# Two transformer blocks in float32: background work timed by a model of the engines, lower parts of weights on VectorE alone

## The chip, the cores and the metric

The kernel runs on one core of one Trainium2 chip. The metric is the device time of one execution in microseconds (us); the median of several runs is compared. The engines of the core each work through a queue of their own, in order: TensorE (PE in the profile; its weight loads are PEld), VectorE (DVE), ScalarE (ACT), GpSimd (POOL) and SyncE (SP), which issues most DMAs.

## The reference

512 tokens of 1024 features pass through two blocks, all in float32:

```python
h = rmsnorm(x, g_pre[l, 0]) * (1 + sc1) + sh1
x = x + 0.5 * gt1 * rmsnorm(swiglu(h, w_gu1[l], w_dn1[l]), g_post[l, 0])
h = rmsnorm(x, g_pre[l, 1]) * (1 + sc2) + sh2
y = token_mixer(h, w_in[l], w_a2[l], b_a[l], b_f[l], g_gla[l], w_pa[l], w_pb[l], w_out[l])
x = x + gt2 * rmsnorm(y, g_post[l, 1])
h = rmsnorm(x, g_pre[l, 2]) * (1 + sc3) + sh3
x = x + 0.5 * gt3 * rmsnorm(swiglu(h, w_gu2[l], w_dn2[l]), g_post[l, 2])
```

The mixer of block 1 is gated linear attention (4 heads) beside a softmax attention with forget gates (16 heads). Block 2 has the same three sub-layers, without the norm on a sub-layer's output; its mixer is a sparse attention of 8 heads (compressed keys, selected and window branch) beside retention of 8 heads. `swiglu` has 2816 hidden features. A last norm gives the result.

## The kernel before

**Products in parts.** Every float32 operand of a weight product is split in two: `hi`, rounded to the format of TensorE's fast pass, and `lo`, the rest. A product is three: hi hi, hi lo, lo hi. Weights come as slabs of 4 x 128 rows by 256 columns (512 KB). For a slab `dma` (L232) loads it to one of 4 buffers `raw`, and `split` (L245) makes its parts: ScalarE casts `hi` (L252), then the *lower part* `lo = raw - hi` (L254) is made by VectorE, or by GpSimd if the job works on half of the tokens (`j_half`). There are 5 pairs of `hi` and `lo`. While a norm has its `hold`, GpSimd's lower parts are kept in `later`, until `catch_up` (L262).

**One order, made in Python.** Instructions are issued engine by engine in the order of the program text, with no reordering. `run` (L298) goes through the list of jobs (a slab and its products); `feed` (L268) loads and splits the slabs ahead. After each three products it calls `background` (L219), which advances Python generators (norms, attention, modulation) whose time has come. Time is `vt`, the sum of what TensorE's products cost; a generator that yields 2.0 goes on when TensorE has been given 2 us more of products. `vt` knows no waits. The numbers are the constants at the top (L24 to L34). `wait_flag` (L226) advances a generator at once where a job needs its result.

**Changes of sub-layer.** The last products of a sub-layer (`tail`) run on tokens 0 to 255 and then on 256 to 511, and so do the first of the next (`head`). So the norm of the first half stands beside the products of the second, and the norm of the second beside the next sub-layer's first half. In block 1 the norm is `residual1` (L525: `rstd`, then for eight chunks of features the scaling L532, the addition to x L538, the square L482 or L485 on ScalarE and its sum L491 in `flush`), then `prenorm` (L494: `rstd` again, then L511, ScalarE's L512 and the lower part L502 for each chunk). In block 2 it is `prenorm` alone. `rstd` (L441) yields Y1, multiplies the sums by ones (TensorE, through `mm`, L184), scales (VectorE, L454), takes the power -1/2 (GpSimd, L456), yields Y2 and spreads the factor over the partitions (TensorE again). The first products of a head go chunk by chunk, each as its chunk of `h` is there.

**Attention.** `softmax_seq` (L1490) serves both softmax attentions: per call the scores of four token tiles (L184), their bias and row minimum on VectorE (L1521), the exponentials on ScalarE (L1524), the scaling by the row sums (L1533), transposes (L189) with copies out on ScalarE and VectorE (L1564, L1562), and the products with the values (`weighted`, L1572). `ret_pair` makes retention for two heads: DMAs that turn rows, rotations (L1858 to L1860), scores, their decay (L1875), values, norm. `gla` (L1266) makes linear attention. All yield fixed numbers between these steps. All products that are not a job's go through `mm` (L183) or `transpose` (L187) to the four banks `bp`; those of jobs through `mmr` (L179) to the banks `mp`. Results of a SwiGLU product are taken out at L566 and L574.

Of the kernel before, what the change touches and what calls it, by code (L numbers as in the profile page):

```python
# [14 lines left out]
ALU = mybir.AluOpType  # L15
# [3 lines left out]
T = 512  # L19
# [4 lines left out]
YR, YP = 1.0, 0.8  # L24
Y1, Y2 = 2.0, 2.0
# [3 lines left out]
S1, SN, S2, S3 = 1, 3, 0.6, 0.4  # L29
KS, NS = 2, 8  # L30
R1, R2, R3 = 4, 1, 0.6
LS, GH = 2, 4
# [57 lines left out]
def packed(name, a, slabs):  # L90
    """The weight a, slab after slab, each with its rows of a chunk on the partitions."""
# [26 lines left out]

class Core:
    def __init__(self, ctx, tc, inp, out):  # L120
        self.tc, self.nc, self.inp, self.out = tc, tc.nc, inp, out
# [11 lines left out]
        self.nraw = self.hold = 0  # L133
# [13 lines left out]
    def alloc(self, rounded=False):  # L147
        """A [128, 512] tile. rounded: for a part of a product's operand (never for other values)."""
# [30 lines left out]
    def mmr(self, out, lhsT, rhs, start, stop):  # L179
        self.nc.tensor.matmul(out, r_(lhsT), r_(rhs), start=start, stop=stop)  # L180
        self.vt += max(0.108, 0.000422 * self.cols(rhs))

    def mm(self, out, lhsT, rhs, start=True, stop=True):  # L183
        self.nc.tensor.matmul(out, lhsT, rhs, start=start, stop=stop)  # L184
# [34 lines left out]
    def background(self):  # L219
        n = 0  # L220
        while self.step(self.vt):
# [19 lines left out]
    def slot(self, old):  # L241
        """A pair of tiles for the parts of a slab that no job from number old on uses."""
        return next((i for i in sorted(range(len(self.his)), key=lambda q: self.until[q]) if self.until[i] < old), None)

    def split(self, j, i):  # L245
# [7 lines left out]
        j_half = j.t1 - j.t0 < T  # L253
        low = lambda e: e.tensor_tensor(r_(l), r, h, op=ALU.subtract)  # L254
# [12 lines left out]

    def feed(self, i):  # L268
        """Loads and splits of the slabs that job i and the next ones use, as far as there is memory."""
# [4 lines left out]
        while moved:  # L274
            moved = False
            if (self.nd < len(L) and self.nd < self.ns + len(self.raws) and L[self.nd] < i + DMA_AHEAD
                    and not any(q.raw is self.raws[self.nraw % len(self.raws)] for q, _ in self.later)):
# [10 lines left out]
    def plan(self):  # L288
        """Which jobs load their slab, and until which job its parts are in use."""
# [8 lines left out]
    def run(self):  # L298
        J = self.jobs
        prev = None  # L300
        for i, j in enumerate(J):
# [11 lines left out]
            if any(q in (j, j.like, prev) for q, _ in self.later):  # L313
                self.catch_up()
# [61 lines left out]
    def turn(g, back=True):  # L376
        """The jobs of a pair by their chunks, from the last to the first or from the first to the last."""
# [6 lines left out]
    def emit_units(self, units, head=0, tail=0, need=None, after=None):  # L384
        """units: lists of pairs. The first `head` and the last `tail` units run on the two halves of the
        tokens one after the other. need: flags (half A, half B); after(t0, t1): called when a half is through."""
# [5 lines left out]
        def both(us):  # L392
            """The jobs of the two halves, the second in the opposite order, so that it finds parts of slabs."""
# [21 lines left out]
                # the first two pairs slab by slab, so that they use the first chunks as soon as they are there  # L415
# [25 lines left out]
    def rstd(self, acc, t0, t1, n=D, eps=EPS):  # L441
        """Generator: sums acc over the partitions, returns 1/sqrt(mean + eps) of each token on all partitions
        (a PSUM bank)."""
        nc = self.nc
        self.flush(acc)
        self.hold += 1
        yield Y1
# [9 lines left out]
        self.hold -= 1  # L457
        if not self.hold:
            self.catch_up()
        yield Y2  # L460
# [16 lines left out]
    def sumsq(self, acc, src, t0, t1, first):  # L477
        """acc += src * src on tokens t0..t1 (square on ScalarE, sum on VectorE, one call later)."""
# [15 lines left out]
    def prenorm(self, acc, h, a, b, t0, t1, flag, spill=False):  # L494
        """Generator: h = (x * a) * rstd + b, split into the parts of h."""
# [13 lines left out]
        for c in range(KC):  # L509
# [6 lines left out]
            yield YP  # L516
# [8 lines left out]
    def residual1(self, y, accy, accx, coef, h, a, b, t0, t1, flag, spill=False):  # L525
        """Generator: x += coef * rmsnorm(y); then the next h from x."""
# [1476 lines left out]
```

## Time and profile before

| | us |
|---|---|
| median of 3 runs (2731.23 to 2737.29) | 2735.96 |
| span of the profiled execution | 2734.5 |
| TensorE busy | 2627.8 |
| VectorE busy | 1403.1 |
| ScalarE busy | 993.9 |
| GpSimd busy | 620.6 |

The profile has no time of its own for that execution beside its span. A line of a group gives the source line, engine, operation, the tile written and those read, shapes, the count, the busy time in us, the mean in ns of one, and then the time for which the engine stood idle just before it, with what released it. A line of waits gives the waiting engine and line, the releaser, the total in us, how often, and the longest. The granted clock (PEclk) is a share of TensorE's full clock.

### The profile page before, as it was taken

How to read it: one execution, taken by the hardware profiler on the slowest of the kernel's cores; microseconds unless marked ns; L12 is line 12 of the kernel's file. 1: busy time of each engine (PE TensorE's matmuls, PEld its weight loads, DVE VectorE, ACT ScalarE, POOL GpSimd, SP SyncE). 2: the span in 40 equal slices, each digit the busy share in tenths (PEclk: the TensorE clock that was granted, in tenths of full speed). 3: DMA queues.
4: the chain of work that ended last, by engine and by line, in shares of the span. 5: the costliest groups of instructions: out<-in, count | busy, mean ns of one | idle time of the engine just before them, and what ended most of it. 6: DMA issues, size and time to landing. Idle time of an engine off the chain costs nothing. (4 is left out here: it accounts for less than half of the span.)

```text
span 2734.5 us, 37488 instructions
## 1 busy us (share of the span) xinstructions
PE 2627.8 (96%) x14965; PEld 2236.6 (82%) x14965; DVE 1403.1 (51%) x2176; ACT 993.9 (36%) x1688; POOL 620.6 (23%) x472
## 2 busy tenths in 40 slices
PE   6999999999999998899998999999999999999998
PEld 4888898888877788888888988899857669998888
DVE  6678446684335535468857333333455454633322
ACT  3332234444344434432234322234345224432223
POOL 4111054430111114411145300044000103520014
PEclk8999999999999999999999999999999999999999
DMA  6677334212333323377843323235310323342323
GB/s 225 220 249 269 101 112 134 79 40 83 126 108 112 97 89 128 115 256 266 277 161 117 111 100 108 94 99 188 101 39 32 123 78 123 116 139 85 108 86 100
DMA packets 128915, 355.12 MB, mean 130 GB/s; under 512 B 16365, under 2 KB 38838, under 8 KB 128740
## 3 DMA queue, kind: packets, MB, share of 16 engines
q1 hardware_dynamic: 110180, 285.54, 31.5%
q0 software_dynamic: 18560, 67.18, 7.2%
q8 instruction: 117, 1.92, 0.3%
q14 instruction: 58, 0.48, 0.1%
HBM read 343.20 MB, written 6.32 MB: 128 GB/s over the span
## 5 line engine op out<-in xcount | busy, mean ns | idle before, releaser
L180 PE MATMUL mp<-t,hi 128*128 128x512 f32 (+1 forms) x7936 | 2047.7, 348 | 11.8 <-DVE t L801 3.6
L180 PEld LDWEIGHTS mp<-t,hi 128*128 128x128 f32 x7936 | 1383.6, 192 | 201.2 <-issue 17.2
L180 PE MATMUL mp<-t,lo 128*128 128x512 f32 (+1 forms) x3968 | 1371.4, 346 | 0.1
L180 PEld LDWEIGHTS mp<-t,lo 128*128 128x128 f32 x3968 | 759.8, 191 | 90.9 <-POOL lo L254 0.3
L252 ACT CAST hi<-raw 128x1024 fp32r<-128x1024 f32 (+2 forms) x493 | 486.1, 991 | 595.8 <-PE mp L180 362.3
L254 DVE TENSOR_TENSOR lo<-raw,hi 128x1024 fp32r<-128x1024 f32 (+3 forms) x316 | 369.4, 1175 | 560.2 <-ACT hi L252 557.7
L254 POOL TENSOR_TENSOR lo<-raw,hi 128x1024 fp32r<-128x1024 f32 (+1 forms) x177 | 401.9, 2285 | 938.5 <-ACT hi L252 919.2
L881 DVE SCALAR_TENSOR_TENSOR big<-big,sc,big 128x1024 f32<-128x1024 f32 x112 | 145.6, 1300 | 22.9 <-DMA big<-in_w_ada 12.5
L180 PE MATMUL mp<-hi,t 128*128 128x256 f32 x704 | 137.5, 291 | 0.0
L574 DVE TENSOR_TENSOR t<-mp,t 128x512 f32<-128x512 f32 (+1 forms) x77 | 44.8, 595 | 152.4 <-PE mp L180 152.4
L180 PEld LDWEIGHTS mp<-hi,t 128*128 128x128 f32 x704 | 114.3, 195 | 6.6 <-issue 5.8
L184 PE MATMUL bp<-t,t 128*128 128x128 f32 (+11 forms) x618 | 111.7, 411 | 6.8 <-DVE t L1875 3.3
L1113 ACT CAST t<-t 128x512 fp32r<-128x512 f32 (+1 forms) x89 | 49.0, 556 | 176.3 <-DVE t L574 160.8
L491 DVE TENSOR_TENSOR t<-t,t 128x256 f32<-128x256 f32 (+1 forms) x109 | 89.9, 827 | 27.2 <-ACT t L485 26.5
L180 PE MATMUL mp<-lo,t 128*128 128x256 f32 x352 | 100.9, 287 | 0.0
L1122 ACT ACTIVATE t<-mp 128x512 f32<-128x512 f32 (+1 forms) x103 | 54.1, 543 | 126.0 <-PE mp L180 123.4
L184 PEld LDWEIGHTS bp<-t,t 128*64 128x64 f32 (+3 forms) x618 | 59.0, 166 | 46.3 <-issue 30.5
L1486 POOL TENSOR_TENSOR big<-big,cmask 128x128 f32<-128x128 f32 x64 | 33.9, 531 | 233.4 <-DMA big<-fdram 233.3
L566 ACT ACTIVATE t<-mp 128x512 f32<-128x512 f32 (+1 forms) x79 | 40.7, 523 | 119.9 <-PE mp L180 119.9
L1524 ACT ACTIVATE t<-t,smx 128x512 f32<-128x512 f32 (+3 forms) x117 | 65.1, 558 | 51.4 <-DVE smx L1521 51.0
L875 POOL DMA_DIRECT2D big<-in_ada_w x72 | 38.8, 539 | 189.0 <-DVE big L881 103.8
L485 ACT ACTIVATE t<-t 128x256 f32<-128x256 f32 (+1 forms) x108 | 44.9, 423 | 97.6 <-DVE t L961 40.4
(269 smaller groups left out, 1774.1 us busy)
## 6 DMA issues: line engine op xcount, KB each, us to landing
raw<-in_w_in SPq DMA_DIRECT2D x112, 512.0 KB
raw<-in_ffn_w_in SPq DMA_DIRECT2D x102, 512.0 KB
raw<-in_w_gu SPq DMA_DIRECT2D x89, 512.0 KB
big<-in_ada_w POOLq DMA_DIRECT2D x72, 512.0 KB, 5.1
big<-in_w_ada POOLq DMA_DIRECT2D x56, 512.0 KB, 4.9
raw<-in_w_dn SPq DMA_DIRECT2D x42, 512.0 KB
raw<-in_ffn_w_out SPq DMA_DIRECT2D x42, 512.0 KB
raw<-in_w_out SPq DMA_DIRECT2D x22, 512.0 KB
```

Source lines behind the costliest of these rows:

```text
L180: self.nc.tensor.matmul(out, r_(lhsT), r_(rhs), start=start, stop=stop)
L184: self.nc.tensor.matmul(out, lhsT, rhs, start=start, stop=stop)
L252: self.nc.scalar.copy(r_(h), r)
L254: low = lambda e: e.tensor_tensor(r_(l), r, h, op=ALU.subtract)
L485: nc.scalar.activation(s[:, t0:t1], src[:, t0:t1], AF.Square)
L491: self.nc.vector.tensor_tensor(acc[:, t0:t1], acc[:, t0:t1], s[:, t0:t1], op=ALU.add)
L566: nc.scalar.activation(s[c, t0][:, t0:t1], banks[n][:, t0:t1], AF.Silu)
L574: nc.vector.tensor_tensor(t[:, tk], banks[n][:, tk], t[:, tk], op=ALU.mult)
L881: nc.vector.scalar_tensor_tensor(acc, raw, self.sc[blk][:, k:k + 1], acc, op0=ALU.mult, op1=ALU.add)
L1113: self.nc.scalar.copy(r_(hi[:, tk]), t[:, tk])
L1122: self.nc.scalar.activation(d[2 * i + n][:, t0:t1], banks[n][:, t0:t1], AF.Copy, scale=scale or 1.0)
L1524: nc.scalar.activation(r, r, AF.Exp, bias=mn[:, c:c + 1], scale=-1.0, accum_out=sm[:, c:c + 1])
```

## The change

Three things change together.

1. Yields. The fixed numbers of norms, softmax, linear attention (in part) and retention go. A class `Times` keeps, for every 128 columns of every tile, when they are expected to be made and last used, and when each engine is free, from a cost for each instruction; `Timed` and `Engine` (not shown in full) pass each instruction on and enter it there. A generator yields until its operands are expected (`when`), a bank `bp` is expected to be free (`bank`), or VectorE is at most 0.7 us ahead of TensorE (`room`).
2. `vt` is TensorE's time by the same model, with its waits; a product of 256 columns counts 0.120 us and not 0.108, and two that use different parts of the array run beside each other.
3. Lower parts. All go to VectorE, in order through `later`: each is issued as soon as its `hi` is expected, or when a job needs it. `hold` is gone. The parts in `startup` (L719) stay on GpSimd.

The other yields (GS, CS, KS, LS, RET_STEP, AD, AP and plain numbers) stay. The rest of the diff takes out comments.

```diff
-YR, YP = 1.0, 0.8
-Y1, Y2 = 2.0, 2.0
...
-S1, SN, S2, S3 = 1, 3, 0.6, 0.4
...
-R1, R2, R3 = 4, 1, 0.6
-LS, GH = 2, 4
+LS = 2
...
+class Times:
+    LAG = {"PE": 0.2, "DVE": 0.15, "ACT": 0.16, "POOL": 0.15}
+    COST = {"DVE": (0.07, 1 / 960), "ACT": (0.09, 1 / 1200), "POOL": (0.12, 2.2e-3)}
+    def __init__(self):
+        self.free = {"PE": 0.0, "DVE": 0.0, "ACT": 0.0, "POOL": 0.0, "SP": 0.0}
+        self.made, self.used = {}, {}
+        self.lock = {"DVE": 0.0, "POOL": 0.0}
+        self.dma = 0.0
+        self.log = None
+    @staticmethod
+    def keys(ap):
+        row = ap.ap[0][0] or 1
+        at = ap.offset % row
+        n = at + sum(abs(s) * (c - 1) for s, c in list(ap.ap)[1:])
+        return [(ap.tensor.tag, q) for q in range(at // 128, n // 128 + 1)]
+    @staticmethod
+    def on_chip(ap):
+        return hasattr(ap, "tensor") and hasattr(ap.tensor, "tag") and ap.space != bass.MemoryType.DRAM
+    def ready(self, *aps):
+        return max((self.made.get(k, 0.0) for a in aps for k in self.keys(a)), default=0.0)
+    def start(self, engine, outs, ins):
+        t = self.free.get(engine, 0.0)
+        for a in ins:
+            for k in self.keys(a):
+                t = max(t, self.made.get(k, 0.0))
+        for a in outs:
+            for k in self.keys(a):
+                t = max(t, self.used.get(k, 0.0))
+        return t
+    def finish(self, outs, ins, end, lag):
+        for a in ins:
+            for k in self.keys(a):
+                self.used[k] = max(self.used.get(k, 0.0), end)
+        for a in outs:
+            for k in self.keys(a):
+                self.made[k] = end + lag
+                self.used[k] = max(self.used.get(k, 0.0), end)
+    def run(self, engine, op, outs, ins, n, two):
+        base, per = self.COST[engine]
+        cost = base + per * n
+        if engine == "POOL" and "memset" in op:
+            cost = 0.1 + n / 1200
+        if engine == "POOL" and n <= 8:
+            cost = 0.7
+        if op in ("scalar_tensor_tensor", "tensor_tensor_reduce", "tensor_tensor_scan"):
+            cost += 0.06
+        if engine == "ACT" and two:
+            cost += 0.09
+        psum = any(a.space == bass.MemoryType.PSUM for a in ins + outs)
+        t = self.start(engine, outs, ins)
+        both = len(ins) > 1 and not psum and not (engine == "ACT")
+        if engine == "DVE" and len(ins) > 1 and sum(a.free_size() > 1 for a in ins) > 1 and not psum:
+            t = max(t, self.lock["POOL"])
+            self.lock["DVE"] = max(self.lock["DVE"], t + cost)
+        elif engine == "POOL" and ins:
+            t = max(t, self.lock["DVE"])
+            self.lock["POOL"] = t + cost
+        self.free[engine] = t + cost
+        self.finish(outs, ins, t + cost, self.LAG[engine])
+        if self.log is not None:
+            self.log.append((engine, op, t, cost))
+    def load(self, engine, out, in_):
+        t = self.free[engine]
+        outs, ins = [a for a in (out,) if self.on_chip(a)], [a for a in (in_,) if self.on_chip(a)]
+        t = self.start(engine, outs, ins)
+        self.free[engine] = t + (0.37 if engine == "SP" else 0.54)
+        n = 1
+        for q in out.shape:
+            n *= q
+        self.dma = max(self.dma, t + 1.6) + 4e-6 * n / 0.33
+        self.finish(outs, ins, self.dma, 0.3)
+        if self.log is not None:
+            self.log.append((engine, "dma", t, 0.4))
...
+    def pe(self, out, lhsT, rhs, cost, part=None):
+        t = self.times.start("PE", [out], [lhsT, rhs])
+        before, at = self.beside
+        if part and before and not part & before:
+            t = max(self.times.start(None, [out], [lhsT, rhs]), at)
+            part = None
+        self.beside = part, t
+        self.vt = self.times.free["PE"] = max(self.vt, t + cost)
+        self.times.finish([out], [lhsT, rhs], t + cost, self.times.LAG["PE"])
+        if self.times.log is not None:
+            self.times.log.append(("PE", "mm", t, cost))
     def mmr(self, out, lhsT, rhs, start, stop):
         self.nc.tensor.matmul(out, r_(lhsT), r_(rhs), start=start, stop=stop)
-        self.vt += max(0.108, 0.000422 * self.cols(rhs))
+        self.pe(out, lhsT, rhs, 0.0135 + self.cols(rhs) / 2400)
     def mm(self, out, lhsT, rhs, start=True, stop=True):
         self.nc.tensor.matmul(out, lhsT, rhs, start=start, stop=stop)
-        self.vt += max(0.214, 4 * 0.000422 * self.cols(rhs))
+        k, m, r, c = lhsT.shape[0], out.shape[0], lhsT.start_partition(), out.start_partition()
+        part = None
+        if k <= 64 or m <= 64:
+            part = frozenset((a, b) for a in range(r // 32, (r + k + 31) // 32) for b in range(c // 32, (c + m + 31) // 32))
+        self.pe(out, lhsT, rhs, max(0.224, 4 * self.cols(rhs) / 2400 + 0.014), part)
     def transpose(self, out, in_):
         p = in_.shape[0]
         self.nc.tensor.transpose(out, in_, self.ident[:p, :p])
-        self.vt += 0.11
+        self.pe(out, in_, in_, 0.11)
+    def when(self, *aps):
+        return max(0.0, self.times.ready(*aps) - self.vt)
+    def room(self, engine="DVE", ahead=0.7):
+        return max(0.0, self.times.free[engine] - self.vt - ahead)
+    def bank(self, n=1):
+        ts = [max(self.times.used.get(k, 0.0) for k in self.times.keys(self.bp[i][:, :])) for i in self.bfree_list[:n]]
+        return max(0.0, max(ts) - self.vt) if len(ts) == n else 0.5
...
     def background(self):
         n = 0
+        self.catch_up()
         while self.step(self.vt):
...
         self.nc.scalar.copy(r_(h), r)
-        j_half = j.t1 - j.t0 < T
-        low = lambda e: e.tensor_tensor(r_(l), r, h, op=ALU.subtract)
-        if not j_half:
-            low(self.nc.vector)
-        elif self.hold:
-            self.later.append((j, low))
-        else:
-            low(self.nc.gpsimd)
-    def catch_up(self):
-        for _, low in self.later:
-            low(self.nc.gpsimd)
-        self.later = []
+        self.later.append((j, h, lambda: self.nc.vector.tensor_tensor(r_(l), r, h, op=ALU.subtract)))
+    def catch_up(self, *jobs):
+        while self.later and (any(q in jobs for q, _, _ in self.later) or not self.when(self.later[0][1])):
+            self.later.pop(0)[2]()
...
-            if any(q in (j, j.like, prev) for q, _ in self.later):
-                self.catch_up()
+            self.catch_up(j, j.like, prev)
...
-        self.hold += 1
-        yield Y1
+        yield max(self.when(acc[:, t0:t1]), self.bank())
         st = self.balloc()
         i0, i1 = t0 // 128, t1 // 128
         for i in range(i0, i1):
@@ -454,10 +600,7 @@
         nc.vector.tensor_scalar(v[:, i0:i1], st[:, i0:i1], 1.0 / n, eps, op0=ALU.mult, op1=ALU.add)
         self.bfree(st)
         nc.gpsimd.tensor_tensor(v[:, 4 + i0:4 + i1], v[:, i0:i1], self.mhalf[:, :i1 - i0], op=ALU.pow)
-        self.hold -= 1
-        if not self.hold:
-            self.catch_up()
-        yield Y2
+        yield max(self.when(v[:, 4 + i0:4 + i1]), self.bank())
...
             old = c, t
-            yield YP
+            yield self.room()
...
             self.sumsq(accx, self.x[c], t0, t1, c == 0)
-            yield YR
+            yield self.room()
...
             S = []
             for lv in range(1, 8):
+                yield max(self.when(ops[hd, lv]), self.bank(2))
...
             for i in (3, 2, 1, 0):
                 w = 128 * (i + 1)
+                yield max(self.when(q, k), self.bank(2))
...
-                yield S1
...
-            yield SN
+            yield self.when(*P)
...
             for j in (3, 2, 1, 0):
                 w = 512 - 128 * j
+                yield max(self.when(*P), self.bank(2))
...
-                yield S2
             self.free(P)
-            yield S3
+            yield max(self.when(*Ts), self.bank())
             cl["use"](PT)
...
-                self.vt -= 2 * 0.000422 * w
...
-        yield R1
+        yield self.when(q, k)
...
+            yield self.bank(2)
...
-            yield R3
         self.free(q, k, dt.pop(u))
-        yield R2
+        yield max(self.when(*Ts), self.bank())
```

More of the change, by code (lines that the diff above doesn't have):

```diff
@@ new lines, with __init__, __getattr__, call @@
+class Engine:
+    def __init__(self, core, engine, name):
+        self.core, self.engine, self.name = core, engine, name
+    def __getattr__(self, op):
+        f = getattr(self.engine, op)
+        times, name = self.core.times, self.name
+        def call(*args, **kw):
+            aps = [a for a in args if hasattr(a, "tensor")] + [kw[k] for k in ("bias", "scale", "in0", "in1") if hasattr(kw.get(k), "tensor")]
+            if op == "dma_start":
+                times.load(name, aps[0], aps[1])
+                return f(*args, **kw)
+            outs, ins = aps[:1], aps[1:]
+            if op == "copy_predicated":
+                ins = aps
+            if op == "tensor_tensor_reduce":
+                outs, ins = [aps[0], aps[-1]], aps[1:-1]
+            if hasattr(kw.get("accum_out"), "tensor"):
+                outs = outs + [kw["accum_out"]]
+            n = 1
+            for q in (ins[0] if ins else outs[0]).shape[1:]:
+                n *= q
+            times.run(name, op, outs, ins, n, any(hasattr(kw.get(k), "tensor") for k in ("bias", "scale")))
+            return f(*args, **kw)
+        return call
@@ L119, with __init__ @@
+class Timed:
+    def __init__(self, core, nc):
+        self.tensor = nc.tensor
+        self.vector, self.scalar = Engine(core, nc.vector, "DVE"), Engine(core, nc.scalar, "ACT")
+        self.gpsimd, self.sync = Engine(core, nc.gpsimd, "POOL"), Engine(core, nc.sync, "SP")
 class Core:
     def __init__(self, ctx, tc, inp, out):
-        self.tc, self.nc, self.inp, self.out = tc, tc.nc, inp, out
+        self.tc, self.inp, self.out = tc, inp, out
+        self.times = Times()
+        self.beside = None, 0.0
+        self.nc = Timed(self, tc.nc)
@@ L132, in __init__ @@
         self.los = [self.sb.tile([128, 4, 256], F32, name=f"lo{i}", tag=f"lo{i}") for i in range(HS)]
-        self.nraw = self.hold = 0
+        self.nraw = 0
         self.outs = None
@@ L276, in feed @@
             if (self.nd < len(L) and self.nd < self.ns + len(self.raws) and L[self.nd] < i + DMA_AHEAD
-                    and not any(q.raw is self.raws[self.nraw % len(self.raws)] for q, _ in self.later)):
+                    and not any(q.raw is self.raws[self.nraw % len(self.raws)] for q, _, _ in self.later)):
                 self.dma(J[L[self.nd]])
@@ L1319, in gla @@
             eb, kd, qe = ops.pop((hd, 0))
+            yield max(self.when(kd), self.bank(2))
             A = self.alloc()
@@ L1334, in gla @@
             self.free(kd)
-            yield 1.0
             S = []
             for lv in range(1, 8):
+                yield max(self.when(ops[hd, lv]), self.bank(2))
                 ps = self.balloc()
@@ L1360, in gla @@
                     S.append(s)
-                yield 1.0
             self.free(q, k, b, eb, kt)
@@ L1373, in gla_head @@
         for e in range(2):
+            yield max(self.when(A, *S, qe), self.bank())
             ps = self.balloc()
@@ L1383, in gla_head @@
             self.sumsq(acc, o[e], 0, T, e == 0)
-            yield 0.5
         self.free(S, A, qe, v)
-        yield GH
         rs = yield from self.rstd(acc, 0, T, n=256)
@@ L1786, in nsa @@
                                         sm[:, 24 + 2 * i:26 + 2 * i, None].to_broadcast([128, 2, 31]), op=ALU.mult)
-            yield 5.0
+            yield self.when(Q)
             for hh in range(2):
@@ L1890, in ret_pair @@
         self.bfree(o)
-        yield 1.0
+        yield max(self.when(ot), self.bank())
         ps = self.balloc()
@@ L1896, in ret_pair @@
         nc.scalar.activation(sq, ot, AF.Square)
-        yield 1.5
+        yield max(self.when(sq), self.bank())
         ps = self.balloc()
@@ L1907, in ret_pair @@
         nc.gpsimd.tensor_tensor(v[:, 8:16], v[:, 0:8], self.mhalf[:, 0:8], op=ALU.pow)
-        yield 2.0
+        yield max(self.when(v[:, 8:16]), self.bank())
         ps = self.balloc()
```

## The prediction

> **What bounds the kernel now.** I begin with the page: its first part (busy time) and second part (40 slices).
>
> ```profile
> span 2734.5 us, 37488 instructions
> PE 2627.8 (96%) x14965; PEld 2236.6 (82%) x14965; DVE 1403.1 (51%) x2176; ACT 993.9 (36%) x1688; POOL 620.6 (23%) x472
> ...
> PE   6999999999999998899998999999999999999998
> ...
> PEclk8999999999999999999999999999999999999999
> ```
>
> TensorE is the bound: 96% busy, while VectorE has 51%. A change of order can only win what TensorE loses. It is idle for 2734.5 - 2627.8 = 106.7 us, and it loses more where the granted clock is below 1. The slices say where: the start, the weak slices at the changes of sub-layer, the end. So the second view is the busy time by stage (columns: window, length, busy time of PE, PEld, DVE, ACT, POOL, granted clock, DMA).
>
> ```profile
> 0.00:68.00 68.00, 41.35 (x167) 33.43 (x168) 47.05 (x63) 22.12 (x41) 27.96 (x22) 0.84 0.70 226
> ```
> ```profile
> 340.00:510.00 170.00, 158.67 (x1120) 146.71 (x1119) 81.72 (x135) 72.33 (x125) 64.65 (x33) 0.92 0.35 112
> 748.00:960.00 212.00, 210.80 (x1214) 158.21 (x1213) 100.00 (x265) 92.75 (x219) 25.37 (x51) 1.00 0.34 108
> 1050.00:1122.00 72.00, 55.14 (x403) 53.89 (x403) 47.65 (x81) 33.41 (x64) 38.72 (x19) 0.88 0.32 103
> 1428.00:1515.00 87.00, 72.23 (x546) 71.62 (x545) 57.91 (x97) 34.58 (x63) 48.48 (x25) 0.88 0.36 120
> 1840.00:1880.00 40.00, 35.63 (x273) 35.23 (x272) 23.52 (x33) 18.14 (x30) 29.13 (x14) 0.91 0.60 211
> 1972.00:2110.00 138.00, 134.03 (x750) 87.36 (x750) 79.64 (x253) 65.73 (x183) 0.00 (x0) 1.00 0.12 40
> 2134.00:2230.00 96.00, 87.70 (x440) 55.61 (x439) 48.27 (x75) 19.77 (x27) 18.06 (x12) 0.96 0.32 99
> 2320.00:2365.00 45.00, 39.17 (x298) 38.56 (x298) 28.97 (x43) 20.56 (x34) 25.44 (x12) 0.92 0.35 118
> 2652.00:2734.50 82.50, 72.94 (x570) 70.45 (x568) 22.31 (x45) 28.53 (x49) 35.35 (x19) 0.97 0.30 96
> ```
>
> I count a stage's loss as idle time plus (1 - clock) x length; that counts clock lost while idle twice, so it is a little high. Changes of sub-layer with a residual (block 1): 340:510 loses 11.3 + 13.6 = **24.9**, 1050:1122 16.9 + 8.6 = **25.5**, 1428:1515 14.8 + 10.4 = **25.2**. Without one (block 2): 1840:1880 **8.0**, 2320:2365 **9.4**. Retention, 2134:2230: **12.1**. The two softmax stages, 748:960 and 1972:2110, lose only **1.2** and **4.0**. The end loses 12.0; the start 37.5, and it yields at no fixed number and is not edited. So the change can work on about 93 us at the five changes of sub-layer, 12 in retention, little elsewhere.
>
> Third view: TensorE's waits (waiting line, releaser, total, times, longest).
>
> ```profile
> PE bp L184 <- DVE t L491: 39.9, 8, 6.1
> ...
> PE bp L184 <- DVE t L1875: 6.8, 2, 3.5
> ...
> PE bp L184 <- DVE big L491: 4.3, 1, 4.3
> ```
>
> L184 behind L491 is the first product of a norm, ones times the sums of squares: nine times, 44.2 us, TensorE stood at it because `yield Y1` released it after 2 us of TensorE's time while VectorE was still adding. TensorE's queue is in order, so weight products that needed nothing stood behind. Each such stall also costs clock. Two cuts, around a norm's stall and around a wait for the DMA of w_a2:
>
> ```profile
> 1068.00:1074.00 6.00, 0.72 (x7) 0.52 (x5) 5.27 (x6) 3.51 (x9) 4.24 (x2) 0.96 0.29 87
> 1074.00:1080.00 6.00, 5.21 (x24) 5.21 (x25) 1.66 (x4) 1.75 (x2) 4.27 (x4) 0.50 0.26 89
> ```
> ```profile
> 478.00:485.00 7.00, 4.91 (x27) 3.30 (x26) 4.36 (x5) 2.82 (x4) 0.00 (x0) 1.00 0.70 233
> 485.00:492.00 7.00, 7.00 (x18) 3.25 (x17) 0.00 (x0) 1.37 (x2) 0.00 (x0) 0.60 0.27 78
> 492.00:500.00 8.00, 8.00 (x27) 5.80 (x27) 0.00 (x0) 4.49 (x8) 0.00 (x0) 0.50 0.00 0
> ```
>
> Six idle microseconds are followed by six at 0.50. But 2.1 us of idle time in 478:485 are followed by 0.60 and 0.50 as well.
>
> The Trainium skill, "TensorE: Matmul & The Clock Gate", section "What's actually happening", says that the clock halves after an idle window of about 3.4 us. By that rule all of the clock's 39.8 us in the five stages would come back once no stall is that long; the 2.1 us here speak against it, and the sum below doesn't use it.
>
> Why VectorE was late: the timeline of VectorE, GpSimd and TensorE at that place.
>
> ```profile
> 1051.13 0.50 PE L184 MATMUL bp<-ones,t 128*128 128x1 f32 x4
> ...
> 1054.73 0.87 DVE L532 SCALAR_TENSOR_TENSOR t<-t,coef,bp 128x256 f32<-128x256 f32 x2 [2.90 <-PE bp L184]
> ...
> 1056.98 0.42 DVE L538 TENSOR_TENSOR t<-t,t 128x256 f32<-128x256 f32 x1
> ...
> 1058.83 4.95 POOL L254 TENSOR_TENSOR lo<-raw,hi 128x1024 fp32r<-128x1024 f32 x2 [3.25 <-ACT hi L252]
> ...
> 1059.10 2.42 DVE L491 TENSOR_TENSOR t<-t,t 128x256 f32<-128x256 f32 x1 [1.70 <-ACT t L485]
> ```
>
> An addition of 128x256 takes 0.42 us alone and 2.42 while GpSimd makes a lower part: it ends about when GpSimd's first one does.
>
> **The change part by part.** *Lower parts to VectorE.* It removes GpSimd's 177 lower parts (first row, the page) and gives VectorE as many, at up to 1.24 us (second row, groups with shapes apart). The other rows are the groups of 1050:1122 and of 1428:1515.
>
> ```profile
> L254 POOL TENSOR_TENSOR lo<-raw,hi 128x1024 fp32r<-128x1024 f32 (+1 forms) x177 | 401.9, 2285 | 938.5 <-ACT hi L252 919.2
> ```
> ```profile
> L254 DVE TENSOR_TENSOR lo<-raw,hi 128x1024 fp32r<-128x1024 f32 x280 | 345.7, 1240 | 515.5 <-ACT hi L252 513.0 <-PE bp L184 0.9
> ```
> ```profile
> L491 DVE TENSOR_TENSOR t<-t,t 128x256 f32<-128x256 f32 x22 | 19.1, 874 | 7.0 <-ACT t L485 6.9
> L538 DVE TENSOR_TENSOR t<-t,t 128x256 f32<-128x256 f32 x16 | 13.8, 862 | 0.0
> ```
> ```profile
> L254 POOL TENSOR_TENSOR lo<-raw,hi 128x1024 fp32r<-128x1024 f32 x15 | 36.0, 2410 | 20.8 <-ACT hi L252 18.3 <-PE mp L180 2.4
> ```
> ```profile
> L491 DVE TENSOR_TENSOR t<-t,t 128x256 f32<-128x256 f32 x26 | 22.9, 882 | 2.2 <-ACT t L485 2.0
> L538 DVE TENSOR_TENSOR t<-t,t 128x256 f32<-128x256 f32 x16 | 11.8, 739 | 0.0
> L502 DVE SCALAR_TENSOR_TENSOR t<-t,mods,t 128x256 fp32r<-128x256 f32 x8 | 9.2, 1151 | 1.2 <-ACT t L512 1.2
> ```
> ```profile
> L254 POOL TENSOR_TENSOR lo<-raw,hi 128x1024 fp32r<-128x1024 f32 (+1 forms) x21 | 47.6, 2284 | 20.9 <-ACT hi L252 20.9
> ```
>
> 1050:1122: VectorE loses the waits for GpSimd, 22 x (0.87 - 0.42) + 16 x (0.86 - 0.42) = 17 us, and gains 15 x 1.24 = 18.6. Its need is 47.65 - 17 + 18.6 = **49**; TensorE's is 72 - 25.5 = **46.5**. 1428:1515: minus 26 x 0.46 + 16 x 0.32 + 8 x 0.71 = 22.8 (0.44 free for L502, half of the pair L532 above), plus 21 x 1.24 = 26: **61**, against 87 - 25.2 = **62**. So VectorE's load hardly changes, and both engines need about the same: neither can be covered wholly by the other. What does change is freedom: a lower part can now fill the time in which VectorE waits for a norm's factor (1051.13 to 1054.73, 3.6 us, four per change of sub-layer).
>
> *Yields by the model.* `rstd` now waits until the sums are expected and a bank is free, so the norm's first product comes after other products, not before them. That takes the stall out of the middle of a half; what is late next is the first product of the next sub-layer, which needs the whole norm, that is VectorE. So I price these stages by VectorE, at 80% of its time: it has 66% now (47.65 of 72, 57.91 of 87), and the 14.4 us of four factors, half covered, would leave 49 / (49 + 7) = 87%. 1050:1122: 49 / 0.8 = 61, gain **11**. 1428:1515: 61 / 0.8 = 76, gain **11**. 340:510: the stretch at w_a2 has 2.1 + 2.8 + 4.0 = 8.9 us of its loss, which nothing edited here touches; of the other 16 the same share, 44%: **7**. Bounds: nothing, or all 67 us. Block 2 has no residual chain and VectorE only 59% and 64% busy: I take 60% of 17.4, **10** (0 to 17).
>
> *Retention.* The scores were issued R1 = 4 us after the rotations, while VectorE stood at the DMAs of the turned rows, so TensorE stood at L1875. With `when(q, k)` it multiplies weights meanwhile: 6.8 us and part of the clock's 3.8, **8** (0 to 12). The rotations' own DMAs still wait on SP behind weight loads, and weight parts behind them on VectorE; the five pairs of parts cover that.
>
> *Softmax, linear and compressed attention.* Fixed numbers left 5.2 us of waits in two stages, so there is only to lose: the model releases a product when it expects its operand, and errors become waits. Nearest rows: the score's eviction of 128x512.
>
> ```profile
> L1521 DVE DVE_READ_ACCUMULATOR2_ANT smx<- 128x1 f32 x128 | 10.6, 83 | 0.0
> ...
> L1521 DVE CUSTOM_DVE_ANT_0 t<-bp,big 128x512 f32<-128x512 f32 x16 | 10.4, 688 | 20.5 <-PE bp L184 20.0 <-issue 0.3
> ```
>
> The model has 0.07 + 512/960 + 0.06 = 0.66 us for these 0.77: 0.11 short. Sixteen calls have ten yields each; if a third of 160 bind, 53 x 0.11 = **6 lost** (all: 18; none, and the old waits gone: 5 won). Linear attention I take at nothing, ± 4: weight products stand beside it.
>
> *Elsewhere.* In the stages of whole tokens lower parts leave VectorE's queue until their upper parts are expected; TensorE doesn't wait there, so nothing. The first slabs' parts in `startup` stay on GpSimd. At the end the chain that ended last has
>
> ```profile
> 2712.15 4.75 POOL lo L254 x2
> ```
>
> so 4.75 - 2 x 1.24 = **2** (0 to 5).
>
> **Sum:** 11 + 11 + 7 + 10 + 8 - 6 + 2 = 43; 2734.5 - 43 = 2691.5 for a span. The median of the runs, 2735.96, is 1.5 above the profiled span, so 2693.
>
> **The rivals.**
> - *Better cover.* Lower parts fill VectorE's waits, and TensorE's own need decides at the changes: 85% of 67 and of 17.4 back, 57 + 15 + 8 + 2 - 3 = 79: **2657**. For it: 24 of 72 us of VectorE are idle in 1050:1122. Against it: the equal needs.
> - *The stall moves.* VectorE's chain is the bound and its time in it unchanged, so TensorE stands at the first product of the next sub-layer instead of at the sums: block 1 gives nothing, block 2 half of 10, retention 8, softmax -6: 7 won, **2729**. For it: 17 us of waits out, 18.6 of parts in. The Trainium skill, "Perfetto Trace Analysis", section "Optimizing Scalar/DVE Operations", has this rule: VectorE and GpSimd share a read port, so moving work between them might not help. The waits of 2.42 us agree.
> - *VectorE's queue in the wrong order, slower.* A job that is due forces its lower parts out at once, and each holds a norm's next step for 1.24 us, on the engine that all wait for. It decides where VectorE's share in these stages falls under today's 66%. At 60%: 49 / 0.6 = 82 (+10), 61 / 0.6 = 102 (+15), the first +7, softmax +6, block 2 nothing, retention -8: +30, **2766**. Against it: norms yield when VectorE is 0.7 us ahead.
> - *The model doesn't move the sums.* It has 0.07 + 256/960 = 0.34 us for L491's 0.42, so it believes VectorE done early; if its error is as large as the fixed number's, all stays: **2736**.
>
> **How the numbers follow.** Chances: forecast 0.46 (2670 to 2715), better cover 0.17, the stall moves 0.17, no move 0.05, slower 0.15. The range 2650 to 2748 leaves out part of the first rival and of the slower one. About 0.2% is what a measurement of this kernel can tell from no change, 5.5 us: of "the stall moves" 0.05 falls within it, with 0.05 of "no move". Faster 0.75, same 0.10, slower 0.15.
>
> **What would show it.** Right: L184 behind L491 falls from 44 us to under 15; L491 and L538 at 0.42 to 0.5 us; POOL under 230 us; VectorE near 1450; 1050:1122 shrinks by about 11 us with a clock above 0.9. Wrong: waits of L180 for L502 or for lower parts of L254 in their place; waits of L184 and L189 for L1521, L1533 or L1564 above 15 us; L1875 unchanged.

## The result and the profile after

The changed kernel takes 2658.73 us (median of 4 runs, 2655.86 to 2659.56) against 2736.62 us before: a ratio of 0.9716 (95% interval 0.9702 to 0.9729), 78 us less. The profiled span went from 2734.5 to 2657.7 us, 76.8 less. The page of the changed kernel, first and second part:

```profile
span 2657.7 us, 37379 instructions
...
PE 2598.7 (98%) x14965; PEld 2221.9 (84%) x14965; DVE 1472.2 (55%) x2353; ACT 1000.3 (38%) x1688; POOL 229.0 (9%) x295
...
PE   6999999999999999999999999999999999999998
...
PEclk8999999999999999999999999999999999999999
```

TensorE has the same 14965 products and is busy for 98%. The weak slices at the changes of sub-layer are gone, and 177 instructions and 392 us have left GpSimd. In this kernel every instruction of VectorE, ScalarE and GpSimd passes through one wrapper, so all have its line, L226 (L214 for DMAs); TensorE's L317, L321 and L330 are what L180, L184 and L189 were. Tiles tell the groups apart. TensorE's waits now:

```profile
PE bp L321 <- DVE t L226: 13.2, 7, 5.2
PE mp L317 <- DVE t L226: 8.7, 6, 3.6
PE bp L321 <- POOL small L226: 6.1, 8, 3.2
...
PE mp L317 <- DVE lo L226: 2.9, 1, 2.9
```

Of the 44 us at the norms' first product nearly nothing is left: some 10 us of the first row are the sums in `startup`, which the kernel before has too.

Both kernels have the same 12960 weight products in the same order, so the start of product number k in both traces says where time was won. The table gives the gain of the span between two such products, in us; the names are those stretches of the kernel before that the prediction used.

| stretch | products | gain |
|---|---|---|
| start | 0 to 500 | -6.4 |
| 340:510, change with residual | 1500 to 2249 | 16.8 |
| linear attention | 2249 to 3000 | 1.1 |
| softmax attention of block 1 | 3000 to 4250 | -0.2 |
| 1050:1122, change with residual | 4250 to 5100 | 15.1 |
| 1428:1515, change with residual | 6500 to 7250 | 20.1 |
| 1840:1880, change | 8500 to 9200 | 6.9 |
| sparse attention and retention | 9300 to 10400 | 12.6 |
| 2320:2365, change | 10600 to 11250 | 9.0 |
| end | 12250 to 12959 | 2.0 |

So 68 us come from the five changes of sub-layer. One of them, products 4500 to 5100, by the windows of equal work, before and then after:

```profile
1050.05:1149.70 99.65, 82.79 (x634) 81.54 (x633) 57.96 (x106) 45.37 (x85) 48.05 (x23) 0.91 0.30 96
```
```profile
1038.80:1123.30 84.50, 78.80 (x634) 77.39 (x633) 61.19 (x126) 45.35 (x85) 6.27 (x7) 0.98 0.41 132
```

VectorE's busy time hardly changes (58.0 to 61.2 us), as 20 parts came from GpSimd and the waits behind its parts went; TensorE's idle time falls from 16.9 to 5.7 us and its clock rises from 0.91 to 0.98. The groups of VectorE in the second window:

```profile
L226 DVE TENSOR_TENSOR lo<-raw,hi 128x1024 fp32r<-128x1024 f32 x20 | 24.4, 1222 | 8.1 <-ACT hi L226 8.1
L226 DVE TENSOR_TENSOR t<-t,t 128x256 f32<-128x256 f32 x38 | 15.1, 422 | 5.1 <-ACT t L226 5.0
```

An addition takes 422 ns, where the two groups of 1050:1122 had means of 874 and 862 before. And VectorE stood only 8.1 us at upper parts that ScalarE had not made, in spite of 20 more parts in its queue. That number turns out to matter most.

### The profile page after: what moved, and what is told of

It is laid out like the page before. It is cut to its first block, busy times and chain, and to the rows that moved or that the text cites. A ratio compares the mean times of both kernels' runs of the same rounds, so it can differ in the third digit from the quotient of the medians.

```text
span 2657.7 us, 37379 instructions
## 1 busy us (share of the span) xinstructions
PE 2598.7 (98%) x14965; PEld 2221.9 (84%) x14965; DVE 1472.2 (55%) x2353; ACT 1000.3 (38%) x1688; POOL 229.0 (9%) x295
## 4 chain that ended last, share of the span: by engine, by line
PE 87%; DVE 5%; issue 4%; ACT 2%; POOL 1%; DMA 1%; SPq 0%; DVEq 0%; POOLq 0%; ACTq 0%
PE mp L317 79%; PE bp L321 7%; DVE t L226 4%; ACT t L226 2%; PE bp L330 1%; DVE lo L226 1%; POOL small L226 0%; DMA t<-in_w_ada 0%; SPq L214 0%; POOL t L226 0%; DMA t<-in_x 0%; ACT hi L226 0%; DMA raw<-in_w_gu 0%; POOL smx L226 0%; PE bp L317 0%
## 5 line engine op out<-in xcount | busy, mean ns | idle before, releaser
L317 PE MATMUL mp<-t,hi 128*128 128x512 f32 (+1 forms) x7936 | 2027.6, 346 | 11.1 <-DVE t L226 8.7
L317 PEld LDWEIGHTS mp<-t,hi 128*128 128x128 f32 x7936 | 1375.7, 190 | 198.7 <-issue 12.1
L317 PE MATMUL mp<-t,lo 128*128 128x512 f32 (+1 forms) x3968 | 1366.2, 344 | 2.9 <-DVE lo L226 2.9
L226 DVE TENSOR_TENSOR lo<-raw,hi 128x1024 fp32r<-128x1024 f32 (+2 forms) x493 | 568.9, 1163 | 595.8 <-ACT hi L226 592.0
L317 PEld LDWEIGHTS mp<-t,lo 128*128 128x128 f32 x3968 | 753.5, 190 | 93.7 <-DVE lo L226 3.3
L226 ACT CAST hi<-raw 128x1024 fp32r<-128x1024 f32 (+3 forms) x501 | 492.2, 988 | 584.5 <-PE mp L317 373.7
L226 DVE TENSOR_TENSOR t<-t,t 128x256 f32<-128x256 f32 (+4 forms) x386 | 201.8, 549 | 69.3 <-ACT t L226 61.6
L226 ACT ACTIVATE t<-mp 128x512 f32<-128x512 f32 (+1 forms) x183 | 97.7, 541 | 299.5 <-PE mp L317 299.4
L226 ACT ACTIVATE t<-t 128x256 f32<-128x256 f32 (+3 forms) x252 | 112.5, 483 | 128.0 <-DVE t L226 105.7
L226 DVE SCALAR_TENSOR_TENSOR big<-big,sc,big 128x1024 f32<-128x1024 f32 x112 | 143.6, 1282 | 18.4 <-DMA big<-in_ada_w 9.3
L226 POOL TENSOR_TENSOR small<-small,mhalf 128x2 f32<-128x2 f32 (+1 forms) x23 | 27.3, 1187 | 1369.9 <-DVE small L226 1369.9
L226 ACT CAST t<-t 128x512 fp32r<-128x512 f32 (+1 forms) x106 | 59.3, 566 | 204.0 <-DVE t L226 201.5
L317 PE MATMUL mp<-hi,t 128*128 128x256 f32 x704 | 134.9, 289 | 0.0
L317 PEld LDWEIGHTS mp<-hi,t 128*128 128x128 f32 x704 | 113.4, 195 | 5.4 <-issue 4.9
L226 DVE TENSOR_TENSOR t<-mp,t 128x512 f32<-128x512 f32 (+1 forms) x106 | 64.8, 621 | 91.0 <-PE mp L317 91.0
L321 PE MATMUL bp<-t,t 128*128 128x128 f32 (+12 forms) x638 | 114.6, 411 | 0.0
L317 PE MATMUL mp<-lo,t 128*128 128x256 f32 x352 | 100.8, 286 | 0.0
L321 PEld LDWEIGHTS bp<-t,t 128*64 128x64 f32 (+4 forms) x638 | 60.4, 167 | 36.7 <-issue 25.9
L226 ACT ACTIVATE t<-t,smx 128x256 f32<-128x256 f32 (+3 forms) x122 | 67.5, 554 | 39.8 <-DVE smx L226 39.6
L317 PEld LDWEIGHTS mp<-lo,t 128*128 128x128 f32 x352 | 68.8, 195 | 0.4
L226 ACT COPY t<-bp 128x512 f32<-128x512 f32 (+3 forms) x85 | 38.7, 461 | 76.4 <-PE bp L330 45.1
L330 PEld LDWEIGHTS bp<-ident,t 128*128 128x128 f32 (+2 forms) x344 | 40.0, 143 | 27.6 <-issue 10.4
```

What stands on the lines that cost most here:

```text
L226: return f(*args, **kw)
```

## The experiments

Three things changed together. Theory A: the engine, GpSimd's parts hold up VectorE's norm. Theory B: the yields, the norm's first product no longer stands in TensorE's queue too early. Theory C came with the fourth run: the instant at which a lower part is put into VectorE's queue. Each run has its own ratio to the kernel before; gains by stretch are counted as in the table, and "the changes" are its five rows with that word (changed kernel: 68). The kernel before, run beside each of them again, had medians from 2731.82 to 2736.62 us. So a difference of less than some 5 us between two runs is not certain from the times alone; where it lies is read from the stretches, each of one trace.

**Lower parts on GpSimd again.**

```diff
-        self.later.append((j, h, lambda: self.nc.vector.tensor_tensor(...)))
+        eng = self.nc.gpsimd if j.t1 - j.t0 < T else self.nc.vector
+        self.later.append((j, h, lambda: eng.tensor_tensor(...)))
```

> The changed kernel (2658.7 us) with the lower parts of half-token jobs on GpSimd again, still issued when expected, and held back while a norm waits for its power. Yields stay by the model. Theory A (GpSimd's parts hold up VectorE's norm, and taking them away is what pays): most of what the five changes of sub-layer gave comes back, 35 us or more of the 68 us that they gave, so 2694 or more; the additions of 128x256 in them have a mean over 0.7 us again. Theory B (the yields pay: the norm's first product no longer stands at the head of TensorE's queue too early): under 15 us come back, 2674 or less, though the additions are as slow as before, since TensorE now multiplies weights meanwhile.

2697.18 us (ratio 0.987, interval 0.9853 to 0.9886). The changes gain 34 and not 68. Two groups of products 4500 to 5100:

```profile
L226 DVE TENSOR_TENSOR t<-t,t 128x256 f32<-128x256 f32 x38 | 28.1, 773 | 8.1 <-ACT t L226 8.0
...
L226 DVE SCALAR_TENSOR_TENSOR t<-t,mods,t 128x256 fp32r<-128x256 f32 x16 | 12.9, 804 | 1.5 <-ACT t L226 1.5
```

Additions are back at 773 ns. As theory A said, by number: the engine is worth 34 us at the changes, with model yields and issue by the model in place. But half of the gain stays.

**The norms' fixed yields.** 2.0 and 2.0 in `rstd`, 0.8 and 1.0 between chunks, in the changed kernel.

> The changed kernel with the fixed yields of the norms (2.0 and 2.0 in rstd, 0.8 and 1.0 between chunks); lower parts on VectorE, the other yields by the model. Theory A: VectorE keeps up without GpSimd's parts, so 2.0 us is nearly late enough and at most 15 us are lost, 2674 or less. Theory B: TensorE stands at the sums again, some 4 us each and half of the clock after it, and 35 us or more are lost, 2694 or more.

2672.02 us (0.9776, 0.9761 to 0.979): 13 us more. The changes still gain 59. Theory B falls as the main cause; the norms' yields are worth about 9 us at the changes. TensorE stands at the norms' sums again, but for 15.9 us and not 44 (its products with `ones` in 100:2700, this run first, then the changed kernel):

```profile
L321 PE MATMUL bp<-ones,t 128*128 128x1 f32 x92 | 13.2, 253 | 15.9 <-DVE t L226 15.9
```
```profile
L321 PE MATMUL bp<-ones,t 128*128 128x1 f32 x92 | 12.1, 241 | 2.5 <-DVE t L226 2.5
```

**The first slabs' lower parts at once.**

```diff
                 self.feed(0)
+                while self.later:
+                    self.later.pop(0)[2]()
```

> The changed kernel, with the lower parts of the first slabs issued at once in startup and not kept until the first job runs. In the changed kernel the first 250 weight products end 6.4 us later than before, with a wait of 2.9 us for a lower part and the clock at half after it. If that delay of issue is the cause: 6 us less, 2652 to 2654. If it is something else (the order of loads, chance): within 1 us of 2658.7.

2652.55 us (0.9705, 0.969 to 0.9719); the start gains 0.0 and not -6.4, all else is as it was. In the changed kernel VectorE's timeline at that place is

```profile
81.78 1.37 DVE L226 TENSOR_TENSOR t<-bp,t 128x512 f32<-128x512 f32 x2 [8.84 <-PE bp L317]
83.16 1.37 DVE L226 TENSOR_TENSOR t<-t,t 128x512 fp32r<-128x512 f32 x2
84.44 4.63 DVE L226 TENSOR_TENSOR lo<-raw,hi 128x1024 fp32r<-128x1024 f32 x4
```

Here VectorE idled for 8.84 us and made four parts after that, when the first job was due: nothing in `startup` calls `catch_up`. With the edit they stand before the outputs of the first products and are made in that gap. The 6.4 us are not the same in every run: with the same instructions up to product 500, the run with retention's yields (below) loses 2.7 there.

**The kernel before, with every lower part on VectorE, and nothing else.**

```diff
-        if not j_half:
+        if True:
             low(self.nc.vector)
```

> The kernel before with one edit: every lower part on VectorE, issued at once behind its upper part; all yields fixed, as before. Theory A: the changes of sub-layer gain 35 us or more of 68, 2700 or less. Theory B: the release of the sums is as it was, and VectorE's queue also stands at upper parts not yet made: no gain or a loss, 2730 or more.

2735.42 us (1.0017, 1.0007 to 1.0027): no gain. Theory A alone falls here: additions of 128x256 (those of the sums) have a mean of 420 ns in this run and nothing is won. The groups with shapes apart show what came in place of the slow additions, first row; the second is the same group of the changed kernel.

```profile
L254 DVE TENSOR_TENSOR lo<-raw,hi 128x1024 fp32r<-128x1024 f32 x433 | 532.2, 1234 | 742.7 <-ACT hi L252 740.0 <-PE bp L184 0.9 <-DMA t<-xdram 0.3
```
```profile
L226 DVE TENSOR_TENSOR lo<-raw,hi 128x1024 fp32r<-128x1024 f32 x433 | 529.9, 1232 | 567.3 <-ACT hi L226 563.8 <-DMA t<-xdram 0.3
```

VectorE stands at upper parts for 740 us, not 564. The same 433 instructions of the same length, put into the queue at another time. In products 4500 to 5100, beside a norm, it stands there for 27.5 us against 8.1 (first row), and TensorE's stall at the sums is as long as before (second row, the whole run):

```profile
DVE lo L254 <- ACT hi L252: 27.5, 20, 3.0
```
```profile
PE bp L184 <- DVE t L491: 45.6, 8, 7.4
```

**At once, in the changed kernel.**

```diff
-        self.later.append((j, h, lambda: self.nc.vector.tensor_tensor(...)))
+        self.nc.vector.tensor_tensor(r_(l), r, h, op=ALU.subtract)
```

> The changed kernel with every lower part on VectorE, but issued at once behind its upper part, as the kernel before did; all yields by the model. Theory C (VectorE's in-order queue: a part issued before its upper part is there holds up the norm behind it, so when it is issued decides): most of the gain at the changes of sub-layer goes, 30 us or more of 68, so 2685 or more, and VectorE's idle time at upper parts rises from 592 to over 700 us. Theory A alone (only the engine matters) with model yields: within 10 us of 2658.7.

2748.48 us (1.0053, 1.0036 to 1.007): 90 us more than the changed kernel, and 14 more than the kernel before beside it. The changes stand at -18, and VectorE's waits for upper parts at 719.8 us. VectorE's timeline in a residual, this run first, then the changed kernel at a like step:

```profile
1070.23 0.75 DVE L226 TENSOR_TENSOR t<-t,t 128x256 f32<-128x256 f32 x2
1072.06 1.23 DVE L226 TENSOR_TENSOR lo<-raw,hi 128x1024 fp32r<-128x1024 f32 x1 [1.08 <-ACT hi L226]
...
1074.46 0.75 DVE L226 TENSOR_TENSOR t<-t,t 128x256 f32<-128x256 f32 x2
1076.30 2.36 DVE L226 TENSOR_TENSOR lo<-raw,hi 128x1024 fp32r<-128x1024 f32 x2 [1.08 <-ACT hi L226]
```
```profile
1053.56 0.75 DVE L226 TENSOR_TENSOR t<-t,t 128x256 f32<-128x256 f32 x2
1054.23 1.22 DVE L226 TENSOR_TENSOR lo<-raw,hi 128x1024 fp32r<-128x1024 f32 x1
1055.37 1.09 DVE L226 TENSOR_TENSOR t<-t,t 128x256 f32<-128x256 f32 x3
```

A part that stands directly behind its upper part makes VectorE wait for ScalarE's cast, 1.08 us, before it works 1.23; the norm behind it waits for both. In the window of products 4500 to 5100 (1059.4:1162.6 here) VectorE stood 23.6 us at upper parts against 8.1, and the window is 18.7 us longer. TensorE waits for what VectorE makes late (the changed kernel has 13.2 and 8.7 in these rows):

```profile
PE bp L321 <- DVE t L226: 43.0, 9, 10.3
PE mp L317 <- DVE t L226: 30.8, 20, 3.5
```

With parts at once the model's yields win nothing in all: with the old yields (the run above) the time was 3 us above the kernel before, with these it is 14 above. The reason was not separated.

**All fixed yields in the changed kernel.** Norms, softmax, linear attention and retention have their old numbers; parts are issued when expected.

> The changed kernel with the fixed yields of the norms, softmax, linear attention and retention put back; lower parts on VectorE and issued when expected, time counted with waits as in the changed kernel. Theory A with C: the changes of sub-layer keep 50 us or more of 68, retention loses its 12: about 2685. Theory B: 2715 or more.

2685.14 us (0.9817, 0.9803 to 0.9832). The changes keep 57. The other loss is in linear attention, 9 us against the changed kernel, perhaps because the old numbers now count time with waits; that is not shown. The expected 2685 was met by luck: retention was to lose its 12 and kept 10.9 of the 12.6.

**Retention's fixed yields alone.**

> The changed kernel with retention's fixed yields alone put back. If the yields give the 12.6 us of the stages of sparse attention and retention: 10 to 13 us back, 2669 to 2672, and the wait for the scores' decay is there again. If the parts that no longer stand in VectorE's queue give it: within 3 us of 2658.7.

2657.48 us (0.9717, 0.9703 to 0.9732): the same as the changed kernel. Its stretch gains 10.6 of 12.6, and the wait at the decay doesn't come back; TensorE's only waits in 2080:2180 are

```profile
PE bp L321 <- POOL smx L226: 1.4, 2, 0.7
PE bp L321 <- DVE t L226: 0.5, 1, 0.5
```

So retention's yields are not needed for it. But the run doesn't show that they give nothing, since the parts' later issue may stand in for them. Other runs tell. In retention's own part of the stretch, products 10000 to 10400, the changed kernel gains 13.0 and this run 11.0. The kernel before with all parts on VectorE at once gained 2.3, and has the wait at the decay:

```profile
PE bp L184 <- DVE t L1875: 5.5, 2, 3.0
```

With the model's yields and parts at once it was 11.1, and no wait of TensorE there adds up to more than 1.6 us. With old yields and each part 2.0 us later (next run) it was 12.2. So either is enough, the yields or the later issue, and the two don't add.

**The kernel before with one number.** All its yields and its count of time; each part on VectorE, 2.0 us of TensorE's time after its upper part was issued.

```diff
-        if not j_half:
-            low(self.nc.vector)
-        ...
+        self.later.append((j, self.vt + 2.0, low))
...
+        while self.later and (any(q in jobs for q, _, _ in self.later) or self.later[0][1] <= self.vt):
+            self.later.pop(0)[2](self.nc.vector)
```

> The kernel before with all its fixed yields and its count of time; every lower part on VectorE, but issued 2.0 us of TensorE's time after its upper part (or when a job needs it), by that one number and no model. Theory A with C: this has both what matters, 40 us or more of 68 at the changes of sub-layer, 2695 or less. If the model's instants are needed: 2715 or more.

2674.66 us (0.9781, 0.9766 to 0.9796): 60 of the 78 us, with no model at all; the changes gain 57. TensorE's stall at the sums, which the bare move had left at 45.6 us, falls with the old yields in place (first row; L483 is what L491 was), and so does VectorE's wait for upper parts in products 4500 to 5100 (second row):

```profile
PE bp L184 <- DVE t L483: 11.5, 8, 2.8
```
```profile
DVE lo L255 <- ACT hi L253: 7.5, 5, 2.6
```

Theories A and C together, then. The move alone gives nothing. The later issue alone, with parts left on GpSimd and old yields, was not run; with the model's yields it gave 35 (first run).

**Half-token jobs at once, the rest when expected.**

> The changed kernel with the lower parts of half-token jobs issued at once on VectorE and those of whole-token jobs issued when expected. If it is the half-token jobs' parts that hold up the norms: the changes of sub-layer lose as in the run with all at once (they stood at -18 us against the kernel before, the changed kernel at +68), so 2730 or more, while the attention stages keep their gain. If the whole-token parts around them do it: 2690 or less.

2749.46 us (1.0059, 1.0044 to 1.0074). The changes stand at -22, the stretch of sparse attention and retention keeps 12.7. The harm is done by the half-token jobs' parts, which are made beside the norms.

**2.0 us earlier, and 2.0 us later, than expected.**

```diff
-            ... or not self.when(self.later[0][1])):
+            ... or self.when(self.later[0][1]) <= 2.0):
```
```diff
-            ... or not self.when(self.later[0][1])):
+            ... or self.times.ready(self.later[0][1]) + 2.0 <= self.vt):
```

> The changed kernel with each lower part issued up to 2.0 us of the model's time before its upper part is expected. If the exact instant matters: 20 us or more lost, 2679 or more. If anything near it does: 2669 or less.

> The changed kernel with each lower part issued 2.0 us of the model's time later than expected, or when a job needs it. If the parts stand ready well ahead of their use, nothing is lost: within 4 us of 2658.7. If lateness costs as much as earliness: as much more as in the run with 2.0 us earlier.

Earlier: 2690.39 us (0.9843, 0.9828 to 0.9859), 32 more. Later: 2647.18 us (0.9687, 0.9671 to 0.9703), 11.5 *less*, which neither expectation had (7 by the distances of both to the kernel before beside them; the changes gain 81.5 and not 68). VectorE's waits for upper parts are 486 us in the whole run against 592, and products 4500 to 5100 take 76.8 us:

```profile
1034.80:1111.60 76.80, 76.00 (x635) 75.60 (x634) 60.54 (x126) 45.71 (x85) 6.27 (x7) 1.00 0.44 139
```

TensorE stands for 0.8 us there at full clock, VectorE has the same work. So the model's instant is still too early, at least here; the reason stays open. Delays other than 2.0 were not tried.

**Both edits that helped.** First slabs at once, all others 2.0 us later.

> The changed kernel with both edits that helped: first slabs' lower parts at once in startup, all others 2.0 us later than expected. If the two gains (6 us and 12 us) are in different places and add: 2640 to 2643. If the later issue only moved work away from what startup delays: 2646 or more.

2641.98 us (2640.38 to 2645.17), ratio 0.9673 (0.9657 to 0.9689): the start gains 0.0 and the changes 81.5, so the gains are in different places and add. This beats both kernels, the changed one by 17 us (12 by the distances to the kernel before).

## Why the prediction was right or wrong

The direction and the range held (2650 to 2748). The forecast of 2693 did not: 43 us were forecast and 78 came, which is the time of the rival "better cover", 2657. Its mechanism, TensorE's own need as the limit, holds at four of the five changes. That its sum came within 2 us is partly luck: block 1 gave 52 us and not 57, the stretch with retention 12.6 and not 8, and the start lost 6.4.

- *What bounds the kernel* was read rightly: 93 us to be won at the changes of sub-layer, of which 68 came; waits at the sums and half the clock; VectorE's additions of 2.42 us behind GpSimd.
- *"So I price these stages by VectorE, at 80% of its time"* is the step that failed. These are windows of the changed kernel with nearly the same work as 340:510, 1050:1122 and 1428:1515:

```profile
346.40:499.60 153.20, 152.20 (x1121) 141.57 (x1120) 88.81 (x165) 72.72 (x125) 4.66 (x4) 0.97 0.38 124
1038.70:1095.60 56.90, 51.20 (x404) 49.78 (x403) 46.59 (x99) 34.42 (x66) 6.27 (x7) 0.97 0.41 127
1401.60:1468.50 66.90, 65.90 (x550) 65.49 (x549) 53.24 (x112) 33.89 (x61) 3.95 (x3) 1.00 0.44 146
```

VectorE is busy for 82% and 80% of the second and third, as assumed, but that is luck: in the third TensorE is idle for 1.0 us at full clock, so its own need sets the time and VectorE's share follows from it. Only in the second is TensorE idle for more, 5.7 us. VectorE's need was too large besides, 53 and not 61 in the third: of 21 parts three were half as long (0.69 us) and three more fall outside the window now, which makes 5 of the 8 us. And 340:510 gave 16.8, not 7: I held 44% to be the share that returns there too, and nearly all of the 16 did. In block 2 15.8 returned, not 10.
- *"VectorE's load hardly changes"* was right, 58.0 to 61.2 us, and *"what does change is freedom"* named the mechanism, but only as time to be filled while a factor is on its way. The runs show more: a part issued before its upper part is there costs VectorE its own 1.2 us and 1.1 of waiting. I took the move to VectorE and the instant of issue as one edit. The move alone is worth 0 (2735.42), the model's instants and yields with half-token parts on GpSimd 35 us, the move and a plain delay 60.
- *The slower rival*, lower parts ahead of a norm's next step in VectorE's queue, is a real mechanism with a smaller price than the 30 us I gave it: with parts issued at once the kernel takes 2748 and 2749, 14 and 17 us over the kernel before beside it. Its trigger is another than I wrote: not a job that is due, but an issue before the upper part is made. Later issue keeps it away, by the model or by one number. The rule of the Trainium skill that moving work between VectorE and GpSimd might not help ("Perfetto Trace Analysis", "Optimizing Scalar/DVE Operations") held for the move alone, 2735.42 against 2732.52, and not for the move with later issue. Its reason, the shared port, is not what kept the move alone from paying: the additions did become fast (420 ns), and waits for upper parts took the place of what they won.
- *Yields by the model* were to take away the stall at the sums, and it fell from 44 us to 2.5. But most of it goes without them: 11.5 us are left with all old yields and a plain delay, 15.9 with the norms' numbers in the changed kernel, and 47.6 (45.6 and 2.0 in two rows) where the parts are only moved. So the late VectorE was the cause more than the early release by 2 us. The norms' yields are worth 9 us at the changes. The new count of `vt` was never taken back alone; the run with one number keeps the old count and has 60 of the 78 us.
- *Retention*: 8 forecast, 12.6 measured with sparse attention, 13.0 of it in retention. The mechanism I named is real: with the model's yields alone (parts at once) 11.1 came and the wait at the decay was gone. But the later issue does the same without them (11.0 and 12.2 with retention's old numbers), which I didn't foresee.
- *Softmax*: -6 forecast, -0.2 measured in block 1 and -0.5 in sparse attention (products 9300 to 10000). The model's 0.11 us per score did not show up as waits of that size.
- *Elsewhere*: I took the start as not edited, and it lost 6.4 us. The parts of the first jobs are split inside `startup` and now wait in `later`, which nothing there empties. GpSimd under 230 us, VectorE near 1450 and 2 us at the end came as forecast (229, 1472, 2.0).

## What to carry to other kernels

On an engine with an in-order queue, when an instruction is issued can be worth more than which engine runs it: here 90 us lay between two programs with the same instructions on the same engines in another order. Look in the profile for an engine's idle time before a group and what ended it; if that engine has other work that someone waits for, put the waiting instruction later, up to the point where its user waits. One number may do most of it (60 of 78 us here), and in this kernel an instant slightly late cost less than one slightly early: 2 us early cost 32, 2 us late won 11.5. Edits can also stand in for each other, as in retention: that taking one back loses nothing doesn't show that it gives nothing alone.

## What the runs showed of the hardware

Starts that match to the instruction can differ by some us. The changed kernel and the run with retention's numbers have the same instructions on all engines up to product 500 and the same wait of 2.9 us for a lower part, and product 500 starts at 178.7 us in the one and 174.2 in the other. In 66:73 the clock was granted to 0.52 in the changed kernel and to 1.00 in the other run (first and second row), and some waits before differ too.

```profile
66.00:73.00 7.00, 7.00 (x22) 5.80 (x22) 4.32 (x7) 2.25 (x3) 2.62 (x2) 0.52 0.00 1
```
```profile
66.00:73.00 7.00, 7.00 (x33) 5.74 (x32) 4.08 (x5) 3.31 (x4) 3.69 (x4) 1.00 0.19 50
```

After the wait of 2.9 us the changed kernel had

```profile
82.00:86.00 4.00, 1.09 (x5) 0.63 (x4) 3.99 (x6) 2.27 (x5) 0.00 (x0) 1.00 0.09 26
86.00:95.00 9.00, 9.00 (x34) 7.21 (x34) 3.07 (x3) 2.10 (x2) 0.00 (x0) 0.81 0.62 204
```

so here 2.9 us of idle time were followed by a lower clock. Shorter waits need not be: the run with retention's numbers stood 2.4 us for VectorE in 60:66, and its clock in 66:73 is 1.00. So the 2.1 us at w_a2, which the prediction took as enough, don't show it: 485:492 has only 18 products, those of 16 rows among them, and that may have had a part. Gains of a few us in a stretch with such a wait should be read from several runs.
